# RWKV in units of 128 tokens on two lanes in place of 256 on one, in a two-layer hybrid decoder

## The chip, the cores and the metric

The kernel runs on one core of a Trainium2 chip. The metric is device time in microseconds of that core: the median of several executions of the whole program. A core has TensorE (PE in the profile: a row for matmuls and one, PEld, for the weight loads that overlap them), VectorE (DVE), ScalarE (ACT), GpSimd (POOL) and the queue SP that issues the DMAs. Each engine works off its own list of instructions in order; semaphores make it wait for the others. TensorE runs at one of two levels, 1.2 or 2.4 GHz; the profile's "granted clock" is the mean share of the higher one.

## The reference: what is computed

Two decoder layers run over a prompt of 2,048 tokens and over a sample group of 8 sequences of 8 tokens that shares the weights. A layer projects the normed input once and hands parts of it to four recurrent mixers (retention, HGRN, GLA, RWKV-7), each with four heads of 64. Their gated outputs are joined, go through `w_out`, and a cross attention to 256 memory tokens follows.

```python
def mixer(h, l, pos, st, v_first, P):
    proj = h @ P['w_in'][l]
    p_ret, p_hgrn, p_gla, p_rwkv = jnp.split(proj, ...)
    ...
    out = jnp.concatenate([o_ret, o_hgrn, o_gla, o_rwkv], axis=-1) @ P['w_out'][l]

def rwkv7_scan(r, w, k, v, kk, a, s0):     # S is (heads, 64 values, 64 keys)
    def step(S, inp):
        rt, wt, kt, vt, kkt, at = inp
        sa = jnp.einsum('bhvk,bhk->bhv', S, kkt)
        S = (S * wt[:, :, None, :] - sa[..., None] * (kkt * at)[:, :, None, :]
             + vt[..., None] * kt[:, :, None, :])
        return S, jnp.einsum('bhvk,bhk->bhv', S, rt)
```

The change cuts the prompt's RWKV recurrence into other pieces; the recurrence itself stays.

## The kernel before

The prompt is worked off in blocks of 512 tokens, four to a layer. In this text block 1.2 is layer 1, block 2; there are eight, from 0.0 to 1.3. In each layer the first block also carries projections of the sample, its RWKV and its GLA, the second block its HGRN, retention and gates (`TURN`).

**Stages of a block.** `block` projects the RWKV inputs, runs RWKV (`R_rwkv`), projects and runs GLA, HGRN and retention; `gates` projects the gates; `finish` multiplies by `w_out` and does the cross attention. The projections and `w_out` are the dense matmuls: 24 to a PSUM tile, 128 rows by 512 or 256 columns, in 32-bit words split into a high and a low part (the tiles `whl`, `act`, `oh`, `ol`). Weights come from DRAM for each block.

**RWKV.** `R_rwkv` takes a unit of 256 tokens, two units to a block, one after the other: they share the tiles of the pool `wk1`, which has one buffer for each name. Inside a unit the tokens lie in chunks of 64. A run of elementwise work on DVE and ACT makes the decays and keys; `invert` inverts the chunks' triangular matrices by doubling in four levels; then come the chunk products and a short serial chain over the chunks through the state `H`. One level of `invert` is: PE transposes `X`; ACT and DVE copy `X` into the block-diagonal tile `Xb` (L947, L949); PE multiplies (`Xb,XB`); ACT and DVE copy the product out of PSUM into `Wb`; PE multiplies (`Wb,XB`); DVE writes `X` under a mask (L968). A unit of 256 tokens has 8 such matrices side by side, so `X` is 128x256.

**PSUM.** Eight banks are four pools of two: `psd` for the dense matmuls, `psb` for GLA and HGRN, `psa` and `psc` for the rest. `PS` hands RWKV's tiles out by turns from `psa` and `psc` (lane `"ac"`).

**What sets the order.** A scheduler lists the instructions of each engine by priorities (`rank`, the table `PRI`) and readiness. `held` keeps a run of matmuls together: after each group's first it raises the priority of the next ones, up to 12 for the dense groups (`DENSE`) and 48 for all others (`SMALL`). So in the part of a block where RWKV runs, the engine lists interleave RWKV, GLA or HGRN on `psb`, and dense groups of the projections that come later in the block. A dense group that stands there is no longer there to be put beside later work.

Three lines carry the unit:

```python
        nu = 1 if smp else 2          # L996
            for u in range(NT // 2):  # L1372
                R_rwkv(l, pr, st["H"], rk, on["rwkv"], wk, u, vfb)
```

Of the kernel before, what the change touches and what calls it, by code (L numbers as in the profile page):

```python
# [12 lines left out]
I32 = mybir.dt.int32  # L13
# [31 lines left out]
SMALL = 48  # L45
# [12 lines left out]
def shape_constants(seq, past):  # L58
# [69 lines left out]
    c["reset"] = np.broadcast_to((np.arange(256) % 64 != 0).astype(f), (128, 256)).copy()  # L128
    c["resets"] = np.broadcast_to((np.arange(SN) % SL != 0).astype(f), (128, SN)).copy()
    return c  # L130


@with_exitstack
def decoder(ctx, tc, I, C, O):
# [74 lines left out]
    run = [SMALL, 0, None]  # L209
# [183 lines left out]
    def group(out, pairs):  # L393
        n = len(pairs)
        run[:] = DENSE, 0, None
        for i, (a, b) in enumerate(pairs):
            mm(out, a, b, i == 0, i == n - 1)
        run[:] = SMALL, 0, None

# [196 lines left out]
    def outputs(seg, score, v, qd, S, NG, NC, kT, tot, wp, eps, center, evac, state_out=None):  # L596
# [316 lines left out]
    def invert(NA, smp, wp):  # L913
# [10 lines left out]
        pair = wp.tile([128, ng * 256], F32, name="XB", tag="kk")  # L924
        ND = pair[:P, :m * 32].rearrange("p (q n) -> p q n", q=m)
        XB = pair[:, m * 32:m * 32 + ng * P].rearrange("p (g b n) -> p g b n", g=ng, b=nb)
        out = wp.tile([128, m, 64], F32, name="XT", tag="wt2")
        flat = lambda x: x.rearrange("p q n -> p (q n)")
        four = lambda x, g: x[:, 4 * g:4 * g + 4]
# [13 lines left out]
        def diagonal(dst, src, n):  # L943

            for b in range(n):
                if b % 2:
                    V.tensor_copy(dst(b), src(b))  # L947
                else:
                    A.activation(dst(b), src(b), AF.Copy)  # L949

        def turned():
            pt = PS("r")[:, :ng * P]
            for g in range(ng):
                tr(pt[:, g * P:(g + 1) * P], flat(four(X, g)), P)
            diagonal(lambda b: Xb[blk[b], :, b, :], lambda b: X[blk[b]], nb)
            A.activation(XB.rearrange("p g b n -> p (g b n)"), pt, AF.Copy)
        for li in range(1, 3 if smp else 5):
            turned()
            pw = PS("r")[:, :ng * P].rearrange("p (g b n) -> p g b n", g=ng, b=nb)
            for g in range(ng):  # L960
# [3 lines left out]
            pz = PS("r")[:P, :m * 32].rearrange("p (q n) -> p q n", q=m)  # L964
            for g in range(ng):
                for b in range(nb):
                    mm(flat(four(pz, g))[blk[b]], XB[:, g, b, :], flat(Wb[:, g, b]))
            V.copy_predicated(X, bc(lmask[:P, li].unsqueeze(1), [P, m, 32]), pz)  # L968
# [6 lines left out]
        low = wp.tile([128, ng * 2, 64], F32, name="XL", tag="rx")  # L975
        G.tensor_copy(low[:, :, 32:64], bc(K["I32"].unsqueeze(1), [128, ng * 2, 32]))
        pw = PS("r")[:, :ng * 64].rearrange("p (g e n) -> p g e n", g=ng, e=2)
        for g in range(ng):
            for q in range(4):
                mm(pw[blk[q], g], NA[:, 4 * g + q, 0, 32:64], Xb[:, 4 * g + q, 0:4:2, :])  # L980
        for q in range(4):
            V.tensor_copy(Wb[blk[q], :, 1:4:2, q, :], XB[blk[q], :, 1:4:2, :])
        A.activation(low[:, :, 0:32], pw.rearrange("p g e n -> p (g e) n"), AF.Copy)
        pz = PS("r")[:, :m * 32].rearrange("p (q n) -> p q n", q=m)
        for g in range(ng):
            for e in range(2):
                mm(flat(four(pz, g))[64 * e:64 * e + 64], low[:, 2 * g + e, :], flat(Wb[:, g, 2 * e + 1]))
# [3 lines left out]
    def R_rwkv(l, seg, Hst, d, on, wp, hb, vf):  # L991
# [4 lines left out]
        nu = 1 if smp else 2  # L996
        P = 64 * ne
        n = nu * P
# [151 lines left out]
        if not smp:  # L1150
            Z = wp.tile([128, m, 2, 64], F32, name="Z", tag="EA")
            A.activation(Z[:, :, 1, :], pk, AF.Copy)
            ps = PS("t").rearrange("p (u i g d) -> p u i g d", u=nu, i=2, g=2)
            for u in range(nu):
                for i in range(2):
                    tr(ps[:, u, i].rearrange("p g d -> p (g d)"), al[:, i, u * 128:(u + 1) * 128], 128)
            A.activation(Z[:, :, 0, :].rearrange("p (g q) d -> p g q d", g=2), ps.rearrange("p u i g d -> p g (u i) d"), AF.Copy)
# [4 lines left out]
            for p in range(2):  # L1162
                A.activation(U[:, p * nq:(p + 1) * nq].rearrange("p q a b -> p q (a b)"), ps[p], AF.Copy)
# [882 lines left out]
```

## Time and profile before

| | us |
|---|---|
| median of three executions (lowest, highest) | 3620.43 (3615.89, 3628.23) |
| the profiled execution, its own time | 3610.52 |
| its span, first to last instruction | 3608.7 |
| PE busy | 3342.4 (93%) |
| PEld busy | 2834.0 (79%) |
| DVE busy | 2069.8 (57%) |
| ACT busy | 1254.4 (35%) |
| POOL busy | 538.4 (15%) |

The mean granted clock over the span is 0.956. A block takes between 350 and 520 us. The text cuts each block in three: the **RWKV stretch** (on PE, from the first low-rank matmul of RWKV, `sm,w` or `dn_v,rwv`, to the transposes of RWKV's last output tile, `fpack,wosb`), the **middle** (from there to the first `w_out` matmul, `whl,oh`: what is left of GLA, HGRN, retention, the sample and the gates) and the rest. Busy times are unions of the instructions' spans, and the end of a matmul is modelled, so a busy PE need not be PE at its peak.

### The profile page before, as it was taken

To read this page: it belongs to the slowest core of one execution; us is meant where nothing else is said; L and a number is where in the kernel's file an instruction comes from. 1 tells how busy PE (TensorE), PEld (TensorE's weight loads), DVE (VectorE), ACT (ScalarE), POOL (GpSimd) and SP (SyncE) were. 2 spreads that over 40 slices of the span, in tenths; PEclk is the share of its full clock that TensorE was granted. 3 is DMA by queue.
4 is the path that set the end of the run, shared out by engine and by line. 5 is a ranking of instruction groups with operands and counts; after the bars stand their busy time and mean duration, and the time that the engine had idled before them with its cause. 6 is when DMAs were issued, how large, how long until landed. Compare 5 with 4: busy or idle time off the path is not lost.

```text
span 3608.7 us, 85093 instructions
## 1 busy us (share of the span) xinstructions
PE 3342.4 (93%) x36126; PEld 2834.0 (79%) x36126; DVE 2069.8 (57%) x5631; ACT 1254.4 (35%) x2655; POOL 538.4 (15%) x632
## 2 busy tenths in 40 slices
PE   7898899999999999999999987999979999999998
PEld 5777687777978888888877856878868788877887
DVE  5665654775436744575456456467653467446754
ACT  4442234322243324332344323443322433244323
POOL 3313230111000100011122232211100011000100
PEclk8999799999999999999999977999989999999999
DMA  6424464236552254325543352542545522543255
GB/s 191 169 88 143 119 228 173 86 90 216 194 196 98 82 193 152 124 73 198 173 172 110 119 156 99 207 145 97 146 150 205 170 98 99 192 148 115 81 201 188
DMA packets 241952, 530.74 MB, mean 147 GB/s; under 512 B 66854, under 2 KB 179750, under 8 KB 197542
## 3 DMA queue, kind: packets, MB, share of 16 engines
q1 hardware_dynamic: 241574, 525.31, 42.6%
q8 instruction: 285, 4.67, 0.5%
q14 instruction: 93, 0.76, 0.1%
HBM read 410.10 MB, written 115.16 MB: 146 GB/s over the span
## 4 chain that ended last, share of the span: by engine, by line
PE 71%; DVE 17%; ACT 5%; issue 4%; DMA 3%; POOL 2%; SPq 0%; ACTq 0%; POOLq 0%; DVEq 0%
PE psd L221 38%; PE psa L221 12%; PE psc L221 11%; PE psb L221 4%; PE psa L263 2%; PE psb L263 2%; PE psc L263 2%; DVE rsq L227 1%; DMA wraw<-in_w_in 1%; DVE Sx L622 1%; POOL whl L227 1%; DVE hss L552 1%; DVE sT L755 1%; DVE osb L227 1%; DVE wosb L227 1%
## 5 line engine op out<-in xcount | busy, mean ns | idle before, releaser
L221 PE MATMUL psd<-act,whl 128*128 128x512 f32 (+1 forms) x4032 | 1014.0, 405 | 29.1 <-DVE th L1283 11.9
L221 PEld LDWEIGHTS psd<-act,whl 128*128 128x128 f32 (+1 forms) x4032 | 751.6, 191 | 211.4 <-issue 22.2
L221 PE MATMUL psd<-whl,act 128*128 128x256 f32 x3840 | 537.7, 293 | 12.3 <-POOL whl L227 8.1
L221 PEld LDWEIGHTS psd<-whl,act 128*128 128x128 f32 x3840 | 487.3, 195 | 38.2 <-issue 16.4
L227 POOL TENSOR_TENSOR whl<-wraw,whl 128x1024 fp32r<-128x1024 f32 (+1 forms) x90 | 216.0, 2406 | 354.3 <-ACT whl L349 343.9
L271 POOL TENSOR_TENSOR ri<-ri,mhalf 128x1 f32<-128x1 f32 (+1 forms) x87 | 49.8, 573 | 1129.0 <-DVE ri L270 1116.1
L221 PE MATMUL psd<-whl,oh 128*128 128x256 f32 x1152 | 211.4, 284 | 0.0
L221 PEld LDWEIGHTS psd<-whl,oh 128*128 128x128 f32 x1152 | 177.7, 189 | 1.1 <-issue 0.3
L221 PE MATMUL psd<-whl,ol 128*128 128x256 f32 x576 | 162.7, 283 | 0.0
L349 ACT ACTIVATE whl<-wraw 128x1024 fp32r<-128x1024 f32 (+1 forms) x90 | 94.2, 1048 | 104.5 <-PE psc L221 35.5
L949 ACT ACTIVATE Xb<-X 32x256 f32<-32x256 f32 (+1 forms) x164 | 67.6, 412 | 143.1 <-DVE X L968 101.8
L221 PE MATMUL psb<-dn_hq,dn_hf 64*64 64x32 f32 (+1 forms) x3840 | 86.4, 234 | 30.9 <-DVE dn_hq L227 9.7
L221 PEld LDWEIGHTS psb<-dn_hq,dn_hf 64*64 64x64 f32 x3840 | 76.1, 149 | 46.8 <-issue 37.8
L221 PEld LDWEIGHTS psd<-whl,ol 128*128 128x128 f32 x576 | 108.6, 189 | 0.0
L227 DVE TENSOR_TENSOR x<-x,psd 128x256 f32<-128x256 f32 x72 | 30.3, 421 | 129.4 <-PE psd L221 129.4
L227 POOL TENSOR_TENSOR tot<-tot 128x8 f32<-128x8 f32 (+7 forms) x128 | 37.4, 293 | 409.1 <-DVE dn_gq L227 179.3
L426 ACT ACTIVATE xs<-xn 128x1024 f32<-128x1024 f32 (+1 forms) x34 | 35.9, 1055 | 173.4 <-PE psb L263 143.8
L755 DVE COPY_PREDICATED sT<-upack,psb 128x256 f32<-128x256 uint8 (+1 forms) x200 | 76.7, 428 | 30.6 <-PE psb L221 29.2
L1283 DVE SCALAR_TENSOR_TENSOR th<-th,psd 128x512 f32<-128x512 f32 x48 | 32.3, 686 | 95.1 <-ACT th L1282 95.0
L221 PEld LDWEIGHTS psd<-hts,wraw 128*64 128x64 f32 x1984 | 67.8, 141 | 20.3 <-issue 9.1
L221 PE MATMUL psa<-whl,oh 128*128 128x256 f32 x448 | 82.8, 283 | 0.0
L221 PE MATMUL psc<-whl,oh 128*128 128x256 f32 x448 | 82.7, 282 | 0.0
(776 smaller groups left out, 6844.7 us busy)
## 6 DMA issues: line engine op xcount, KB each, us to landing
whl<-w_w_out SPq DMA_DIRECT2D x56, 1024.0 KB
wraw<-in_w_in SPq DMA_DIRECT2D x76, 512.0 KB
wraw<-in_w_out SPq DMA_DIRECT2D x32, 512.0 KB
w_w_out<-whl SPq DMA_DIRECT2D x16, 1024.0 KB
x<-x SPq DMA_DIRECT2D x32, 512.0 KB
whl<-w_rw_r SPq DMA_DIRECT2D x12, 1024.0 KB
whl<-w_rw_k SPq DMA_DIRECT2D x12, 1024.0 KB
whl<-w_rw_v SPq DMA_DIRECT2D x12, 1024.0 KB
```

The source lines that it names most:

```text
L221: PE.matmul(out, lhsT=lhsT, rhs=rhs, start=start, stop=stop, skip_group_check=True)
L227: e.tensor_tensor(out, a, b, op)
L263: PE.transpose(out, in_, ident[:rows, :rows])
L271: G.tensor_tensor(y, y, mhalf[:P], ALU.pow)
L349: A.activation(hl[:, 0], raw, AF.Copy)
L426: A.activation(out, xt, AF.Square, accum_out=ss[:P])
L552: V.tensor_reduce(ss[:P, :n4], sq[:P, :n4], AX.X, ALU.add)
L622: V.scalar_tensor_tensor(b, a, tot(t, c)[gs], pu[gs, t, c, :], ALU.mult, ALU.add)
L755: V.copy_predicated(out, bc(mk, [P, w, 32 // s, s]), ps)
L949: A.activation(dst(b), src(b), AF.Copy)
L1283: V.scalar_tensor_tensor(th, th, 1.0, x, ALU.add, ALU.mult)
```

## The change

RWKV's unit becomes 128 tokens, four to a block. The units take turns on two lanes: `Turn` gives unit u the tiles and the PSUM pool of lane u % 2 (`psa` or `psc`), each tile half as large as before, so two units can be under way at a time. Their only dependence is the state `H`, which a unit reads near its end. `invert` has 4 matrices in place of 8. `SMALL` goes: all runs of matmuls are held by 12. In the blocks with the sample the state slot `Sx` of GLA and HGRN moves from the mixers' pools into the tile `th` of `dnp`. GLA, HGRN and retention keep their units of 512 (256 in the blocks with the sample).

```diff
-SMALL = 48
...
-    c["reset"] = np.broadcast_to((np.arange(256) % 64 != 0).astype(f), (128, 256)).copy()
+    c["reset"] = np.broadcast_to((np.arange(128) % 64 != 0).astype(f), (128, 128)).copy()
...
+class Turn:
+    def __init__(self, pool, i):
+        self.pool, self.i = pool, i
+
+    def tile(self, shape, dtype, name, tag, bufs=None):
+        return self.pool.tile(shape, dtype, name=name, tag=f"{tag}{self.i}", **({"bufs": bufs} if bufs else {}))
...
-    run = [SMALL, 0, None]
+    run = [DENSE, 0, None]
...
+            elif center:
+                x = wp.tile([128, nt - 1, NC, 128], F32, name="Sx", tag="Sx")
             else:
-                x = wp.tile([128, nt - 1, NC, 128], F32, name="Sx", tag="Sx")
+                x = dnp.tile([128, TB], F32, name="Sx", tag="th", bufs=2)[:, :NC * 128].rearrange("p (t c n) -> p t c n", t=1, c=NC)
...
-        m = NA.shape[1]
-        ng = m // 4
...
-        pair = wp.tile([128, 2, m, 32], F32, name="X", tag="wt1")[:P]
+        pair = wp.tile([128, 2, 4, 32], F32, name="X", tag="wt1")[:P]
...
-            pw = PS("r")[:, :ng * P].rearrange("p (g b n) -> p g b n", g=ng, b=nb)
-            for g in range(ng):
-                for q in range(4):
-                    mm(flat(pw[:, g])[blk[q]], ND[:, 4 * g + q, :], flat(Xb[:, 4 * g + q]))
-            diagonal(lambda q: Wb[blk[q], :, :, q, :], lambda q: pw[blk[q]], 4)
+            pw = PS("r")[:, :P].rearrange("p (b n) -> p b n", b=nb)
+            for q in range(4):
+                mm(flat(pw)[blk[q]], ND[:, q, :], flat(Xb[:, q]))
+            diagonal(Wb, pw, 4)
...
-        nu = 1 if smp else 2
-        P = 64 * ne
-        n = nu * P
+        nu = 1
+        P = n = 64 * ne
...
-            for j in range(ng):
+            for j in range(2):
                 ph = PS("r")[:, :128].rearrange("p (i n) -> p i n", i=2)
...
-            for u in range(NT // 2):
+            for u in range(NT):
+                wp = Turn(wk, u % 2)
                 vfb = None
                 if l > 0:
-                    vfb = wk.tile([128, 2, 256], F32, name="vfb", tag="vT")
-                    dma(vfb, vf[b][:, :, u * 256:(u + 1) * 256])
-                R_rwkv(l, pr, st["H"], rk, on["rwkv"], wk, u, vfb)
+                    vfb = wp.tile([128, 2, 128], F32, name="vfb", tag="vT")
+                    dma(vfb, vf[b][:, :, u * 128:(u + 1) * 128])
+                with on_lane("ac"[u % 2]):
+                    R_rwkv(l, pr, st["H"], rk, on["rwkv"], wp, u, vfb)
```

The engine lists move at three places that the prediction speaks of. In the rows, `fpack,X` is a transpose of `X`, `dn_gq` and `dn_gk` are GLA, `dn_hq`, `dn_hf`, `dn_hv` are HGRN, `Ss`, `sv`, `vx` and `ds_` tiles are the sample, `whl` with `act` is dense; the last number is how many stand in a row.

DVE, one level of `invert` in block 0.1, before:

```order
L947 COPY Wb<-psc 32x8x32 x2
L968 COPY_PREDICATED X<-upack,psa 128x256
L947 COPY Xb<-X 32x8x32 x2
L755 COPY_PREDICATED sT<-upack,psb 128x8x2x16 x2
L227 TENSOR_TENSOR dn_gk<-dn_gk,tot_13403 128x16x16
L227 TENSOR_TENSOR dn_gq<-dn_gq,tot_13403 128x32x16
L947 COPY Wb<-psa 32x8x32 x2
L968 COPY_PREDICATED X<-upack,psc 128x256
L947 COPY Xb<-X 32x8x32 x2
```

and after:

```order
L956 COPY Wb<-psa 32x4x32
L956 COPY Xb<-X 32x4x32 x2
L766 COPY_PREDICATED sT<-upack,psb 128x8x4x8
L956 COPY Wb<-psa 32x4x32
L766 COPY_PREDICATED sT<-upack,psb 128x8x4x8
L956 COPY Wb<-psc 32x4x32
L236 TENSOR_TENSOR dn_gk<-dn_gk,tot_14717 128x32x8
L236 TENSOR_TENSOR dn_gq<-dn_gq,tot_14717 128x64x8
L956 COPY Wb<-psc 32x4x32
L974 COPY_PREDICATED X<-upack,psa 128x128
L974 COPY_PREDICATED X<-upack,psc 128x128
L975 STREAM_TRANSPOSE X<-X 128x128
```

Where one matrix set of 128x256 went through, two of 128x128 go through, with twice the copies and the two lanes' steps mixed.

PE, two levels of the same `invert`, before:

```order
L221 MATMUL psc<-Wb,XB 32x128 x8
L221 MATMUL psb<-dn_gq,dn_gk 64x64 x16
L263 MATMUL psa<-fpack,X 128x128 x2
L221 MATMUL psc<-Xb,XB 32x128 x8
L221 MATMUL psd<-act,whl 128x512 x12
L221 MATMUL psa<-Wb,XB 32x128 x8
L221 MATMUL psb<-dn_gq,dn_gk 64x128 x8
L263 MATMUL psc<-fpack,X 128x128 x2
```

and after:

```order
L230 MATMUL psd<-act,whl 128x512 x12
L272 MATMUL psa<-fpack,X 128x128
L230 MATMUL psa<-Xb,XB 32x128 x4
L230 MATMUL psc<-Wb,XB 32x128 x4
L230 MATMUL psb<-dn_gq,dn_gk 64x64 x14
L272 MATMUL psc<-fpack,X 128x128
L230 MATMUL psc<-Xb,XB 32x128 x4
L230 MATMUL psb<-dn_gq,dn_gk 64x64 x2
L230 MATMUL psd<-act,whl 128x512 x12
L230 MATMUL psa<-Wb,XB 32x128 x4
L230 MATMUL psc<-Wb,XB 32x128 x4
L230 MATMUL psb<-dn_gq,dn_gk 64x64 x14
```

Before, the pools `psa` and `psc` alternate within one unit; now each is a unit of its own, the groups are half as long, and a transpose is followed at once by its own lane's product.

PE in the middle of block 1.0, the second half of HGRN, before:

```order
L221 MATMUL psb<-dn_hq,dn_hf 64x32 x64
L263 MATMUL psa<-fpack,osb 128x128 x4
L221 MATMUL psb<-dn_hq,dn_hf 64x32 x16
L221 MATMUL psb<-dn_hq,dn_hf 64x64 x8
L263 MATMUL psb<-fpack,dn_hf 128x128 x4
L221 MATMUL psb<-dn_hv,ha 64x64 x8
L221 MATMUL psb<-S_hgrn,dn_hq 64x128 x2
L221 MATMUL psb<-dn_hv,sT 64x64 x4
```

and after:

```order
L230 MATMUL psc<-Ss,qx 64x64 x10
L230 MATMUL psa<-vx,gmn 32x512 x2
L230 MATMUL psb<-dn_hq,dn_hf 64x64 x8
L272 MATMUL psa<-fpack,dn_rk 128x128 x4
L230 MATMUL psa<-vx,gmn 32x512 x2
L230 MATMUL psd<-whl,act 128x256 x12
L272 MATMUL psb<-fpack,dn_hf 128x128 x4
L230 MATMUL psd<-whl,act 128x256 x12
L272 MATMUL psc<-fpack,osb 128x64 x2
L230 MATMUL psb<-dn_hv,ha 64x64 x8
```

Before, this half stands behind the sample's mixers with retention alone beside it; now it ends beside the sample's GLA (`vx,gmn`), ahead of retention, with dense groups between.

## Rows read from the trace of the kernel before

**Rows 1.** The page's busy times: engine, us, share, instructions.

```profile
PE 3342.4 (93%) x36126; PEld 2834.0 (79%) x36126; DVE 2069.8 (57%) x5631; ACT 1254.4 (35%) x2655; POOL 538.4 (15%) x632
```

**Rows 2.** Windows: eight RWKV stretches; length, engines' busy us, clock, DMA share, GB/s.

```profile
123.00:299.00 176.00, 160.28 (x2329) 135.71 (x2328) 113.89 (x311) 71.32 (x151) 41.13 (x40) 0.96 0.31 113
620.00:778.00 158.00, 151.19 (x2525) 127.82 (x2524) 115.04 (x321) 63.73 (x135) 13.78 (x28) 1.00 0.23 81
1080.00:1247.00 167.00, 160.46 (x2620) 137.79 (x2617) 117.53 (x337) 58.47 (x128) 17.66 (x30) 1.00 0.23 80
1461.00:1618.00 157.00, 150.71 (x2518) 127.11 (x2517) 114.09 (x321) 63.59 (x135) 14.45 (x30) 1.00 0.23 81
1865.00:2061.00 196.00, 181.29 (x2534) 155.19 (x2534) 122.31 (x336) 77.86 (x163) 48.78 (x43) 0.97 0.34 121
2380.00:2572.00 192.00, 181.96 (x2752) 157.52 (x2750) 134.67 (x382) 72.21 (x150) 21.55 (x37) 0.99 0.32 111
2864.00:3051.00 187.00, 179.37 (x2752) 155.77 (x2751) 133.88 (x377) 67.63 (x144) 21.41 (x36) 1.00 0.29 100
3249.00:3438.00 189.00, 180.84 (x2744) 156.11 (x2742) 136.14 (x377) 70.16 (x146) 20.64 (x34) 0.99 0.28 94
```

**Rows 3.** Windows of the eight middles, in the order of the blocks.

```profile
299.00:489.00 190.00, 158.44 (x1681) 126.86 (x1680) 120.83 (x329) 55.16 (x112) 63.26 (x63) 0.83 0.45 140
778.00:905.00 127.00, 115.80 (x1039) 95.79 (x1039) 74.88 (x233) 27.09 (x56) 22.15 (x26) 0.92 0.65 197
1247.00:1328.00 81.00, 76.90 (x519) 65.67 (x518) 49.33 (x129) 23.46 (x41) 6.72 (x9) 0.98 0.57 198
1618.00:1717.00 99.00, 91.22 (x639) 78.93 (x639) 51.34 (x140) 20.71 (x35) 13.06 (x17) 0.98 0.59 195
2061.00:2248.00 187.00, 151.86 (x1500) 116.90 (x1501) 108.81 (x317) 53.89 (x112) 54.34 (x57) 0.72 0.39 123
2572.00:2691.00 119.00, 93.94 (x833) 73.11 (x834) 61.34 (x184) 23.03 (x50) 16.30 (x21) 0.83 0.51 153
3051.00:3117.00 66.00, 60.85 (x399) 50.37 (x400) 38.34 (x97) 19.46 (x35) 4.82 (x7) 0.95 0.51 184
3438.00:3502.00 64.00, 60.98 (x417) 51.21 (x417) 36.17 (x89) 16.85 (x28) 4.26 (x6) 1.00 0.53 191
```

**Rows 4.** Groups by form: DVE and ACT; count, busy us, mean ns, idle before.

```profile
L227 DVE TENSOR_TENSOR bn<-bn,EA 128x512 f32<-128x512 f32 x16 | 10.9, 682 | 0.0
...
L227 DVE TENSOR_TENSOR ar<-kk,eb 128x256 f32<-128x256 f32 x32 | 13.1, 416 | 0.0
...
L1116 ACT ACTIVATE kT<-psa 128x512 f32<-128x512 f32 x8 | 4.8, 596 | 18.9 <-PE psa L263 14.9 <-issue 4.1
L956 ACT ACTIVATE XB<-psa 128x256 f32<-128x256 f32 x40 | 15.3, 382 | 5.0 <-PE psa L263 4.2
```

**Rows 5.** Chain of waits in `w_out`: start, us, what.

```profile
1357.79 2.85 PE psd L221 x24
1360.64 1.43 PE psa L221 x12
```

**Rows 6.** The same chain inside an RWKV stretch, block 0.3.

```profile
1489.35 1.62 PE psd L221 x12
```

**Rows 7.** Window in block 1.3 with the densest DVE found over 60 us.

```profile
3355.00:3415.00 60.00, 55.72 (x1010) 49.97 (x1007) 53.09 (x149) 24.64 (x56) 7.66 (x12) 1.00 0.23 78
```

**Rows 8.** The chain in the middle of block 1.0, second half of HGRN.

```profile
2202.39 1.14 PE psb L221 x32
2203.52 0.47 DVE sT L755 x2
2203.99 0.33 DVE dn_hf L227
2204.33 0.34 DVE dn_hq L227
```

**Rows 9.** Waits of PE over the whole run: us in total, times, longest.

```profile
PE psc L263 <- DVE osb L227: 13.6, 5, 7.7
```

More of the change, by code (lines that the diff above doesn't have):

```diff
@@ L394, in group @@
         n = len(pairs)
-        run[:] = DENSE, 0, None
+        run[2] = None
         for i, (a, b) in enumerate(pairs):
             mm(out, a, b, i == 0, i == n - 1)
-        run[:] = SMALL, 0, None
+        run[2] = None
     def dense_c(w, act, ps):
@@ L974, in invert @@
         turned()
[L975 to L980, printed above, removed]
-        for q in range(4):
[L982 to L987, printed above, removed]
+        low = wp.tile([128, 2, 64], F32, name="XL", tag="rx")
+        G.tensor_copy(low[:, :, 32:64], bc(K["I32"].unsqueeze(1), [128, 2, 32]))
+        pw = PS("r")[:, :64].rearrange("p (e n) -> p e n", e=2)
+        for q in range(4):
+            mm(pw[blk[q]], NA[:, q, 0, 32:64], Xb[:, q, 0:4:2, :])
+        for q in range(4):
+            V.tensor_copy(Wb[blk[q], 1:4:2, q, :], XB[blk[q], 1:4:2, :])
+        A.activation(low[:, :, 0:32], pw, AF.Copy)
+        pz = PS("r")[:, :128].rearrange("p (q n) -> p q n", q=4)
+        for e in range(2):
+            mm(flat(pz)[64 * e:64 * e + 64], low[:, e, :], flat(Wb[:, 2 * e + 1]))
         A.activation(out[:, :, 32:64], pz, AF.Copy)
@@ L1150, in R_rwkv @@
         if not smp:
-            Z = wp.tile([128, m, 2, 64], F32, name="Z", tag="EA")
+            Z = wp.tile([128, 4, 2, 64], F32, name="Z", tag="EA")
             A.activation(Z[:, :, 1, :], pk, AF.Copy)
[L1153 to L1157, printed above, removed]
@@ L1162, in R_rwkv @@
-            for p in range(2):
-                A.activation(U[:, p * nq:(p + 1) * nq].rearrange("p q a b -> p q (a b)"), ps[p], AF.Copy)
+                    mm(ps[ep, 2 * p + q, :], XT[ep, 2 * p + i, :], Z[ep, 2 * p + q].rearrange("p a b -> p (a b)"))
+            A.activation(U.rearrange("p q a b -> p q (a b)"), ps, AF.Copy)
             R1 = wp.tile([128, 2, n], F32, name="R1", tag="kp")
-            GT = wp.tile([128, 2, ng, 64], F32, name="GT", tag="kk")
-            DB = wp.tile([128, 2, ng, 64], F32, name="DB", tag="rx")
@@ new lines, in R_rwkv @@
+            ipe = [(i, p, e, slice(64 * p, 64 * p + 64), slice(64 * e, 64 * e + 64)) for i in range(2) for e in range(2) for p in range(2)]
+            for i, p, e, hp, ep in ipe:
+                mm(pr[e][hp, i], U[ep, 2 * p + i, 0, :], NA[ep, 2 * p + i, 1:3, :])
+            r4 = lambda x: x.rearrange("p i (e n) -> p i e n", e=2)
+            for e in range(2):
+                tt(V, GT[:, :, e], pr[e][:, :, 1, :], bc(K["I64"].unsqueeze(1), [128, 2, 64]), ALU.add)
+                tt(V, r4(R1)[:, :, e], pr[e][:, :, 0, :], r4(rt)[:, :, e], ALU.add)
@@ new lines, in R_rwkv @@
+            for e in range(2):
+                pg.append(PS("r")[:, :128].rearrange("p (i n) -> p i n", i=2))
+            for i, p, e, hp, ep in ipe:
+                mm(pg[e][hp, i, :], kT[ep, 0, hs(i, p)], vT[ep, 0, hs(i, p)], True, False)
+                mm(pg[e][hp, i, :], bT[ep, 2 * p + i, :], U[ep, 2 * p + i, 1, :], False, True)
+            for e in range(2):
+                tt(V, DB[:, :, e], pg[e], bc(eb[:, :, e, 64:65], [128, 2, 64]), ALU.mult)
+            Hn = wp.tile([128, 2, 2, 64], F32, name="Hn", tag="wt2")
@@ L1184, in R_rwkv @@
             V.tensor_copy(Hn[:, 0], Hst)
-            H = [Hn[:, j] for j in range(ng)] + [Hst]
-            for j in range(ng):
+            H = [Hn[:, 0], Hn[:, 1], Hst]
+            for j in range(2):
                 ph = PS("r")[:, :128].rearrange("p (i n) -> p i n", i=2)
@@ L1234, in R_rwkv @@
         if not smp:
-            o4 = lambda x: x.rearrange("p u (i g n) -> p u i g n", i=2, g=2)
-            pq = [PS("r")[:, :nu * 128].rearrange("p (u i n) -> p u i n", u=nu, i=2) for _ in range(2)]
+            o4 = lambda x: x[:, 0].rearrange("p (i g n) -> p i g n", i=2, g=2)
+            pq = [PS("r")[:, :128].rearrange("p (i n) -> p i n", i=2) for _ in range(2)]
             for q, i, u, e, tk, hp, ep in each(0):
@@ L1637, in w_out @@
                     for t in ts:
-                        run[:] = DENSE, 0, None
                         for n, k in enumerate(ks):
```

73 lines of the change are left out of this document (31 added, 42 removed).

## The prediction, as it was put on record

> **What bounds the kernel now.** I read the page's busy times first [rows 1]: PE is busy 93% of the span and no other engine over 60%, so a change pays if it takes work or waiting off PE. Then I cut every block in three and read windows. In the RWKV stretches [rows 2] the reader is to see that PE is already full: in block 0.2 it is busy 160.5 of 167 us at a granted clock of 1.00, while DVE is busy 117.5. The eight stretches sum to 1422 us (176, 158, 167, 157, 196, 192, 187, 189). The time that PE loses lies elsewhere, in the middles of three blocks that carry the sample [rows 3]. In 1.0 PE is idle for 35 of 187 us and its granted clock is 0.72, so that it ran there partly at 1.2 in place of 2.4 GHz, worth another 52 us (187 x 0.28); in 0.0 the same reading gives 32 and 32 of 190, in 1.1 it gives 25 and 20 of 119. The chain of waits names one cause: the second half of HGRN runs behind the sample, and one of its levels is 1.1 us of small matmuls and then 1.2 us of DVE in which PE has nothing [rows 8]; the 1.1 middle has two long waits for a retention output on DVE, up to 7.7 us [rows 9]. So two halves of a unit that overlap can give little inside the RWKV stretch, where dense groups hide its chain already; what they can give is that the stretch needs fewer dense groups to hide it and leaves them to the middles.
>
> **DVE and ACT: more instructions, the same elements.** By the instruction lists DVE gets 1,496 more, all of RWKV, 187 to a block; ACT gets 760, or 95 to a block. A DVE instruction of 512 elements takes 682 ns and one of 256 takes 416 [rows 4], so one cut in two costs 2 x 416 - 682 = 150 ns more. That is 28 us of DVE in each RWKV stretch, 224 in all. On ACT it is 2 x 382 - 596 = 168 ns, 16 us to a stretch; ACT is busy at most 78 of some 190 us there [rows 2], so I cost that at nothing, and without that cover it would be 16 us to a block. DVE's busy time in the stretches goes from 114, 115, 118, 114, 122, 135, 134, 136 to 142, 143, 146, 142, 150, 163, 162, 164, in sum 1212. How full can DVE be when its list is in order and it waits for PE and ACT? Over a whole stretch it is 0.70 to 0.72 in blocks like 1.2 and 1.3; over the densest 60 us that I found it is 53.1, or 0.885 [rows 7]. With two units and GLA or HGRN to choose from I take the upper end, which gives 160, 162, 165, 160, 169, 184, 183, 185 us as DVE's floors.
>
> The Trainium skill bears on this in its page "Perfetto Trace Analysis", section "Optimizing Scalar/DVE Operations", which argues both ways: larger grouped operations help where the engine is saturated, while breaking instructions up may help where it is not but makes others wait. It puts the fixed cost on SBUF at about 60 ns of engine time and says that the profiled latency is about twice that. The rows' 150 ns is near the double; with 60 ns the stretches would get 11 us of DVE each, DVE would be no floor anywhere, and RWKV would end some 20 us lower in sum. The row decides here.
>
> **PE: the same columns, more switches, other neighbours.** Matmul counts hardly move (112 more, each of them half of one that is gone), so the work is the same. Three things move. First, the dense groups that stand in the RWKV stretches. A dense matmul of 256 columns takes 0.119 us (12 in 1.43) [rows 5], one of 512 is counted double. Counted so, the stretches lose 120, 24, 24, -36, 228, 156, 144, 132 of them, or 14, 3, 3, -4, 27, 19, 17, 16 us, 94 in sum, to the middles. Second, the lists have 409 more rows in the stretches and 161 more in the middles, which is 409 and 161 more changes from one group to another. A change costs nothing in `w_out`, where 12 take 1.43 whatever came before [rows 5], and up to 0.19 in an RWKV stretch, where 12 dense matmuls take 1.62 [rows 6]. I take 0.10, about the middle, since only part of the new changes are beside dense groups: 41 us and 16 us. Third, the half-size groups wait on half-size copies, and `X` is followed at once by its own product; that wait is already in the stretches of before, so I give it no term. PE's floors are then length less what leaves plus the changes: 168, 160, 168, 166, 174, 179, 176, 178.
>
> **The RWKV stretches in sum.** The larger floor of each is 168, 162, 168, 166, 174, 184, 183, 185, in sum 1390. Both engines are now near full and each waits for the other in a fixed order, so I add 4 us to each stretch, somewhat over half of the 6.5 that PE is idle in 0.2 now [rows 2]: 1422. Against 1422 before, that is no change: what leaves, 94 us, is paid back by DVE's floor, the changes and the waiting. The bounds are 1372, if changes and waiting cost nothing, and 1683, if DVE stays at 0.72.
>
> **The middles.** In 1.0 the second half of HGRN ends ahead of retention and beside dense groups, so its own 35 us or so of half-idle time go, and 27 us of dense work come in, into a middle that loses 87 us (35 idle and 52 of clock). Between nothing and the 60 us that are left after that work is placed, I take half, -30; by the same rule 0.0 (64 lost, 14 come in, 50 left) gets -25. In 1.1 the 19 that come in fit into the 45 lost, and dense groups now stand by retention, so I take -8, about half of the two long waits. In 0.1 (10 of clock, 11 idle) and 0.2 (6 in all) the 3 that come in are hidden. 0.3 gives 4 away. In 1.2 and 1.3 the middles are full, losing 8 and 3 us [rows 3], so of 17 and 16 some 9 and 13 us are left over on the path. The changes add 11 outside the terms of 0.0 and 1.0. Sum: -30 - 25 - 8 - 4 + 9 + 13 + 11 = -34. The rest of each block, `w_out` and the cross attention, keeps its order. What `SMALL` did is in the row counts; the moved `Sx` slot takes a tile of the gates and has free time around it, which I cost at nothing; if it made the second HGRN half wait, that is the second rival. The weights that the moved dense groups need are 1 MB for 24 groups and move with them, in middles where the DMA engines are busy 0.39 and 0.45 in 1.0 and 0.0 [rows 3].
>
> **The time.** The profiled execution took 3610.5 us, 10 us under the median of 3620.4. 3610.5 + 0 - 34 = 3576, and beside the median 3586: I say 3585.
>
> **Rivals.** (1) *DVE takes PE's place, slower.* If DVE reaches not 0.85 of the stretches, which the forecast needs (1212 of 1422), but 0.80, halfway between 0.72 and 0.885 [rows 2, 7], the stretches take 1515, 93 more, and the total is +59: 3670 in the profile, 3680 as a median. It decides from a DVE share under 0.83 (1212 / 1456). For it: every unit now runs all its DVE steps in order with the other lane's, and PE's list cannot fill what it did not foresee. Against it: three chains feed DVE where there were two. The page "Perfetto Trace Analysis" of the Trainium skill, in the section named above, warns of this case. Chance 0.32. (2) *The middles hold.* The sample's RWKV, GLA and retention follow each other as before; if they, and not HGRN, set the end in 0.0 and 1.0, only 20 of the 55 us come, and the total is +1: 3611, median 3620. Against it stands the half-idle stretch [rows 8], for it that the sample's chain has no less work. Chance 0.13. (3) *More than forecast.* Changes cost nothing and the two engines never wait for each other: stretches 1372, middles -45, in all -95: 3515, median 3525. For it, `w_out` pays nothing [rows 5]; against it, 1.62 in place of 1.43 [rows 6]. Chance 0.12. The forecast keeps 0.43.
>
> **How the numbers follow.** A measurement of this kernel can tell about 0.3%, 11 us, from no change. The forecast is faster but for 0.03, so faster is 0.40 + 0.12 = 0.52; same is 0.13 and 0.01 of the forecast, 0.14; slower is 0.32 and 0.02, 0.34. The range reaches from 3505, under the third rival's median, to 3695, over the first rival's; beyond it lie DVE shares under 0.79 and a fuller recovery of the middles.
>
> **What would show it.** In the changed profile: DVE busy some 2290 us in all, ACT some 1380; the eight RWKV stretches together near 1422 us with DVE at 0.85 in them; the middles of 1.0 and 0.0 near 157 and 165 us with the clock there over 0.9; the middles of 1.2 and 1.3 some 10 us longer. The forecast is wrong if the stretches sum to over 1456, with PE idle waiting for `X`, `Xb` or `Wb`, or if the middle of 1.0 keeps its low clock.

## The result: slower by half a per cent, and the profile after

The changed kernel takes 3635.4 us, the median of eleven executions; the kernel before takes 3615.9 over eleven that stand beside them. The ratio is 1.0053, with a 95% interval of 1.0039 to 1.0067. The forecast was 3585 and faster.

The page of the changed kernel, busy times (engine, us, share, instructions), against [rows 1]:

```profile
PE 3415.0 (94%) x36350; PEld 2846.7 (78%) x36350; DVE 2267.3 (62%) x7127; ACT 1371.9 (38%) x3415; POOL 554.6 (15%) x712
```

DVE gained 197 us and ACT 118, close to the forecast (2267 where 2290 was said, 1372 for 1380). The next two fences are windows of the changed kernel, in the columns of [rows 2, 3]. First the RWKV stretches of 1.0 and 1.3, and the sum over all eight:

```profile
1878.00:2069.80 191.80, 172.72 (x2303) 135.69 (x2300) 145.60 (x520) 87.06 (x252) 39.75 (x54) 0.87 0.27 91
...
3267.70:3446.60 178.90, 169.07 (x2515) 137.08 (x2514) 143.66 (x514) 80.68 (x237) 19.91 (x42) 1.00 0.25 88
sum 1408.70, PE 1329.15 PEld 1068.84 DVE 1114.34 ACT 634.35 POOL 190.61; mean PE 166.14 PEld 133.60 DVE 139.29 ACT 79.29 POOL 23.83
```

Then the middles of 0.0, 1.0, 1.2 and 1.3, and the sum over all eight:

```profile
300.40:484.70 184.30, 164.08 (x1804) 136.40 (x1803) 123.95 (x322) 58.73 (x117) 65.44 (x60) 0.91 0.47 153
...
2069.80:2256.00 186.20, 166.42 (x1776) 137.51 (x1774) 124.21 (x326) 59.45 (x120) 64.38 (x59) 0.88 0.46 148
...
3052.30:3137.10 84.80, 79.44 (x542) 67.46 (x541) 47.02 (x125) 22.65 (x40) 7.54 (x10) 0.98 0.53 189
3446.60:3536.80 90.20, 85.27 (x686) 72.84 (x685) 50.35 (x144) 20.77 (x35) 6.45 (x8) 1.00 0.45 161
sum 989.90, PE 905.58 PEld 760.31 DVE 613.98 ACT 269.20 POOL 207.45; mean PE 113.20 PEld 95.04 DVE 76.75 ACT 33.65 POOL 25.93
```

The stretches went from 1422 to 1409, the middles from 933 to 990. In 1.0 the clock of the middle rose from 0.72 to 0.88, and the middle is still as long as it was (187 to 186); the stretch ahead of it, at 0.97 before, is now at 0.87.

The experiments are easiest to read by two groups of blocks. The table gives stretch and middle together, from each run's own profile: the two blocks with the sample's RWKV (0.0, 1.0), and the six plain ones. "Room" is explained with e18. A profile is one execution, up to 12 us from its kernel's median, and the kernel before itself has medians from 3611.6 to 3618.3 in the rounds of measurement, so a few us between two rows decide nothing.

| kernel | lanes | hold | room for HGRN | median us | two sample blocks | six plain blocks |
|---|---|---|---|---|---|---|
| before | 1 | 48 | no | 3616 | 749 | 1607 |
| e2 | 1 | 12 | no | 3614 | 734 | 1629 |
| e18 | 1 | 48 | mask | 3580 | 716 | 1602 |
| e3 | 1 | 48 | slot | 3570 | 700 | 1617 |
| e5 | 1 | 12 | slot | 3562 | 690 | 1628 |
| e12 | 1 | 12, HGRN 48 | slot | 3554 | 689 | 1615 |
| e20 | 1 | 12, HGRN 48 | mask | 3549 | 691 | 1610 |
| e15 | 1 | 12, HGRN 48 | no (own tile) | 3597 | 724 | 1616 |
| e19 | 2 | 12 | no | 3644 | 746 | 1649 |
| e6 | 2 | 48 | mask | 3595 | 724 | 1625 |
| e13 | 2 | 12 | mask | 3594 | 696 | 1649 |
| e1 | 2 | 48 | mask, slot | 3595 | 720 | 1626 |
| **changed kernel** | 2 | 12 | mask, slot | 3635 | 742 | 1656 |
| e11 | 2 | 12, HGRN 48 | mask, slot | 3586 | 708 | 1628 |
| e14 | 2 | 12 | mask, own tile | 3595 | 698 | 1650 |
| e16 | 2 | 12, HGRN 48 | mask, own tile | 3592 | 716 | 1624 |

### The profile page after: what moved, and what is told of

Same layout as the page of the kernel before. It is cut to its first block, busy times and chain, and to the rows that moved or that the text cites. A ratio compares the mean times of both kernels' runs of the same rounds, so it can differ in the third digit from the quotient of the medians.

```text
span 3644.3 us, 88156 instructions
## 1 busy us (share of the span) xinstructions
PE 3415.0 (94%) x36350; PEld 2846.7 (78%) x36350; DVE 2267.3 (62%) x7127; ACT 1371.9 (38%) x3415; POOL 554.6 (15%) x712
## 4 chain that ended last, share of the span: by engine, by line
PE 67%; DVE 20%; ACT 4%; issue 3%; DMA 3%; POOL 2%; SPq 0%; ACTq 0%; POOLq 0%; DVEq 0%
PE psd L230 34%; PE psa L230 12%; PE psc L230 11%; PE psb L230 5%; PE psc L272 2%; PE psa L272 2%; DVE rsq L236 2%; PE psb L272 2%; DVE Sx L633 1%; DVE osb L236 1%; DVE hri L292 1%; DVE Wb L956 1%; DVE hss L561 1%; DVE Xb L956 1%; POOL whl L236 1%
## 5 line engine op out<-in xcount | busy, mean ns | idle before, releaser
L230 PE MATMUL psd<-act,whl 128*128 128x512 f32 (+1 forms) x4032 | 998.6, 401 | 19.3 <-DVE carry L539 7.8
L230 PE MATMUL psd<-whl,act 128*128 128x256 f32 x3840 | 551.0, 296 | 3.8 <-ACT whl L358 1.6
L958 ACT ACTIVATE Xb<-X 32x128 f32<-32x128 f32 x324 | 99.3, 307 | 125.3 <-DVE X L974 75.7
L230 PE MATMUL psb<-dn_hq,dn_hf 64*64 64x32 f32 (+1 forms) x3840 | 119.8, 225 | 9.1 <-DVE dn_hq L236 4.1
L230 PEld LDWEIGHTS psb<-dn_hq,dn_hf 64*64 64x64 f32 x3840 | 104.0, 138 | 28.8 <-issue 18.2
L230 PE MATMUL psd<-hts,wraw 128*64 128x64 f32 x1984 | 84.4, 232 | 1.9 <-DVE th L1285 1.9
L956 DVE COPY Xb<-X 32x128 f32<-32x128 f32 x324 | 79.3, 246 | 7.6
```

The costliest lines, as they stand in the source:

```text
L230: PE.matmul(out, lhsT=lhsT, rhs=rhs, start=start, stop=stop, skip_group_check=True)
L956: V.tensor_copy(o, i)
L958: A.activation(o, i, AF.Copy)
```

## The experiments

**One part at a time (e1 to e4).** First the theories were that short holds cut GLA's and HGRN's runs (S), or that the lanes cost the time (L).

e1 puts the long holds back:

```diff
-    run = [DENSE, 0, None]
+    run = [SMALL, 0, None]      # SMALL = 48; group() sets DENSE and back, as before
```

> The changed kernel with one part undone: runs of small matmuls are held by 48 again, as before the change (PE's list has 6,357 rows; 6,553 in the changed kernel, 5,985 before). Theory S (the splitting of GLA's and HGRN's runs costs the time): in the changed kernel the matmuls of dn_gq,dn_gk and dn_hq,dn_hf take 23.4 us more of PE than before (179.8 against 156.3, from start to start); held by 48 they go back to some 157, and the median falls from 3635 to 3605-3618. Theory L (the lanes cost it, by halved groups that end more often: X, Xb and Wb take 35 us more of PE): the median stays within 8 us of 3635, since PE fills what it gains with waiting for DVE.

Measured: 3594.7, ratio to the kernel before 0.9946 (0.9924 to 0.9968). That is 41 us under the changed kernel, below the range of S and far from that of L.

e2 is the kernel before with the short holds alone, the reverse of that edit.

> The kernel before with that one part alone: all runs of matmuls held by 12, units of 256 on one lane. Theory S: dn_gq,dn_gk and dn_hq,dn_hf take some 20 us more of PE, and the median goes from 3616 to 3630-3640, which is all of the change's loss. Theory L: within 8 us of 3616, because shorter holds also let RWKV's small groups in sooner.

Measured: 3614.4, ratio 0.9994 (0.9976 to 1.0013): nothing, in the range of L. So the holds cost 41 us beside the other parts (e1) and nothing by themselves (e2); neither S nor L says both.

e3 is the kernel before with `Sx` in the `th` tile, as in the diff of the change.

> The kernel before with only the slot Sx of the blocks with the sample moved into a tile of the gates. If the slot is what lets the second half of HGRN stand earlier, the middles of 0.0 and 1.0 (190 and 187 us) get shorter by 5 to 25 us each and the median falls to 3580-3608. If the lanes are what moves it, nothing changes: 3616, within 8 us.

Measured: 3569.9, ratio 0.9885 (0.9849 to 0.992). The part that I had costed at nothing is worth 1.2% alone.

e4 takes the overlap away and keeps the halves:

```diff
-                wp = Turn(wk, u % 2)
+                wp = Turn(wk, 0)
-                with on_lane("ac"[u % 2]):
+                with on_lane("ac"):
```

> The changed kernel with its units of 128 on one lane (the tiles of lane 0 for every unit, PSUM from the two pools by turns as before): halved instructions without overlap. If the overlap is what the halves buy, four serial chains stand in each RWKV stretch where two stood, the stretches (1409 us in sum in the changed kernel) grow by 60 us or more, and the median is 3690 or above. If DVE's count of instructions or PE's changes set the time and not the chains, it stays within 20 us of 3635.

Measured: 4005.3, ratio 1.1075. The eight stretches take 2015 us in sum. In e5 below, which has the same holds and slot and units of 256 on one lane, they take 1377: 86 us to a unit of 256, and here 63 to a unit of 128 (at a mean granted clock of 0.906 over the span, against 0.972). So half the tokens are far from half the time on one lane, and the second lane buys back what the halves lose. Busy times of e4:

```profile
PE 3513.4 (88%) x36350; PEld 2911.7 (73%) x36350; DVE 2270.7 (57%) x7127; ACT 1384.3 (35%) x3415; POOL 549.9 (14%) x712
```

DVE does the same work in e4 as in the changed kernel (2267) and is busy for a smaller share of the span: it waits, it is not full.

**Parts in pairs, and DVE's instructions (e5, e6, e7, e10).** e5 is e3 with the short holds.

> Units of 256 on one lane, with the slot Sx moved and all runs held by 12: the changed kernel without its lanes. Measured so far: the slot alone 3570, holds of 12 alone 3614 against 3612, and with lanes and slot the holds cost 41 us (3595 to 3635). If it is the lanes that make the short holds dear (more groups to change to), this takes 3562-3582. If it is the slot (HGRN then stands beside RWKV, and it is HGRN's long runs that are cut), it takes 3598-3618.

Measured: 3562.4, ratio 0.9854 (0.9827 to 0.9881). That is the range of the lanes: one lane bears short holds with the slot moved, too.

e6 is the changed kernel with long holds and `Sx` back in the mixers' pools.

> The lanes alone: units of 128 on two lanes, runs held by 48, Sx in the mixers' pools as before. If the parts add up, the lanes cost the 25 us here that they cost with the slot moved (3570 to 3595), and this takes 3627-3647. If what I forecast for the lanes holds (they let the second half of HGRN stand earlier and fill the middles of 0.0 and 1.0), it takes 3575-3595.

Measured: 3594.5, ratio 0.9943 (0.9922 to 0.9964). This looked like my forecast for the lanes come true; e19 speaks against it.

e7 is e3 with a wrapper around VectorE in the prompt's RWKV that writes each elementwise operation, copy and transpose of 64 elements or more as two:

```diff
+            for h in range(2):
+                f(out[..., half h], *[the same half of each operand], **k)
```

> The kernel before with Sx moved (3570), and each DVE operation of the prompt's RWKV written as two of half the size: 1,144 more DVE instructions, about 172 us more of DVE's busy time at 0.15 each, PE's matmuls and their groups unchanged. If DVE's added instructions are what the lanes cost, this loses most of the lanes' 25 us: 3585-3600. If the cost is on PE (groups cut in half, X, Xb and Wb ending 133 times where they ended 68), DVE's time is hidden: 3562-3578.

Measured: 3602.0, ratio 0.9956 (0.994 to 0.9971), 32 us over e3 and just above the range of DVE's instructions. Busy times of e3 and then of e7:

```profile
PE 3322.0 (93%) x36126; PEld 2820.1 (79%) x36126; DVE 2080.6 (58%) x5631; ACT 1253.4 (35%) x2655; POOL 536.1 (15%) x632
```

```profile
PE 3339.4 (93%) x36126; PEld 2827.8 (79%) x36126; DVE 2164.1 (60%) x6775; ACT 1255.9 (35%) x2655; POOL 538.9 (15%) x632
```

1,144 more instructions made DVE busy for 84 us more, 73 ns each. By the blocks, the loss is in the two with the sample (700 to 728) and in what follows the middles (1127 to 1136); the six plain ones take 1614 against 1617. So more DVE instructions cost nothing in the plain blocks, where dense groups cover the chain, and they are hardly what the lanes cost there. That they delay a chain with little beside it in the sample blocks is my reading of these times; no run shows it.

e10 has the lanes in blocks 0.1 and 1.1 alone:

```diff
+            two = b == 1
+            nu = 1 if two else 2
-            for u in range(NT // 2):
+            for u in range(NT // nu):
+                wp = Turn(wk, u % 2) if two else wk
```

> The kernel before with Sx moved, and the lanes of 128 in blocks 0.1 and 1.1 alone (units of 256 on one lane in the other six, runs held by 48). Lanes with the slot made 0.1 and 1.1 shorter by 5.5 and 5.3 us and 1.0 and 1.3 longer by 18 and 11 (3595 in all against 3570). If the lanes' worth hangs on the block, this takes 3552-3566, under both kernels and under the slot alone; if those block differences are only work handed on to the next block, it takes 3566-3580.

Measured: 3564.0, ratio 0.9854 (0.9833 to 0.9876), in the range of "the block matters". The interval overlaps that of e3, so the 6 us stay inconclusive.

**The slot beside the lanes (e11 to e16).** e11 holds the prompt's HGRN by 48 in the changed kernel; e12 does the same in e5.

```diff
+                run[0] = 48
                 R_hgrn(l, gr, st["hgrn"], ...)
+                run[0] = DENSE
```

> The changed kernel with the prompt's HGRN alone held by 48 again, all else by 12 (PE's list has 86 rows of dn_hq,dn_hf; 153 in the changed kernel, 93 with every run held by 48). Between these two the matmuls of dn_hq,dn_hf took 75.7 us of PE with long holds and 117.5 with short ones, 42 us, which is all of the 41 us between 3595 and 3635. If HGRN's cut runs are the loss, this takes 3585-3605. If the loss is that short holds no longer let RWKV end sooner once it has two lanes, and HGRN only shows it, this stays at 3620-3640.

> Units of 256 on one lane, Sx moved, holds of 12 for all but HGRN's 48. There short holds made the RWKV stretches 38 us shorter (1416 to 1378) and the middles 40 us longer, with 31 us more for dn_hq,dn_hf. If HGRN's cut runs are what the middles pay, the two can be parted and this takes 3525-3550, the best of all. If the middles grow because what leaves the stretches has to stand somewhere, it stays at 3555-3575.

Measured: e11 3586.3, ratio 0.9937 (0.9913 to 0.9961); e12 3553.8, ratio 0.9841 (0.9822 to 0.9859). Both moved the way of the cut runs, e11 into that range, e12 to a place between its two ranges. The matmuls of HGRN in the page's groups (count, busy us, mean ns, idle before), of e11 and of the changed kernel:

```profile
L230 PE MATMUL psb<-dn_hq,dn_hf 64*64 64x32 f32 (+1 forms) x3840 | 77.4, 222 | 8.2 <-DVE dn_hq L236 4.6 <-DVE dn_hf L851 2.1 <-issue 1.0
```

```profile
L230 PE MATMUL psb<-dn_hq,dn_hf 64*64 64x32 f32 (+1 forms) x3840 | 119.8, 225 | 9.1 <-DVE dn_hq L236 4.1 <-DVE ds_qk L236 2.7 <-DVE dn_hf L851 1.7
```

e13 is the changed kernel with `Sx` back in the mixers' pools.

> The changed kernel with Sx back in the mixers' pools: lanes and short holds without the slot. With long holds the slot was worth nothing beside the lanes (3594.5 without, 3594.7 with it). If that holds with short ones, this takes 3627-3643, like the changed kernel; if the slot's 46 us are still in it, 3660 or more.

Measured: 3594.2, ratio 0.9959 (0.9941 to 0.9976). Its HGRN matmuls take 118.4 us, as cut up as in the changed kernel, and it is 41 us faster, outside both ranges. So the cut runs are not the whole loss, and the slot costs 41 us where one lane gained 42 from it (e3, against the kernel before in its own round). The two profiled executions are 53 us apart, 46 of them in the two sample blocks (742 against 696). With the old slot the short holds cost nothing beside the lanes either (e6 3594.5, e13 3594.2): 24 us more in the plain blocks, 28 less in the sample's.

What the slot does is in the trace of 1.0. ACT's first writes of `th` by HGRN's query projection (L532), and the last writes of GLA's state (the fields after the durations are first and last start); first the changed kernel, then e13:

```profile
L532 ACT ACTIVATE th<-psd x4: 224/408/597, 2029.0 to 2046.2; 128x512 f32<-128x512 f32 x2, 128x64 f32<-128x64 f32 x2
L633 DVE SCALAR_TENSOR_TENSOR S_gla<-Sx,tot,psb x4: 272/280/288, 1950.1 to 2031.5; 64x64 f32<-64x64 f32 x4
```

```profile
L532 ACT ACTIVATE th<-psd x4: 224/411/599, 1975.0 to 1996.4; 128x512 f32<-128x512 f32 x2, 128x64 f32<-128x64 f32 x2
L631 DVE SCALAR_TENSOR_TENSOR S_gla<-Sx,tot,psb x2: 273/280/286, 2004.9 to 2005.2; 64x64 f32<-64x64 f32 x2
```

There are two `th` tiles. GLA's keys `dn_gk` hold one, its `Sx` now holds the other, and the projection, whose PSUM tile is read through `th`, has to wait for GLA: it writes 2 us ahead of GLA's end in the changed kernel and 30 us ahead of it otherwise. The dense groups behind it wait with it: from 100 to 150 us into the stretch of 1.0 PE runs 44 of the prompt's dense matmuls in the changed kernel and 88 in e13. Windows of the changed kernel there, 10 us each, and of e13 at the same distance from the start of the stretch (columns as in [rows 2]):

```profile
1998.00:2008.00 10.00, 8.85 (x98) 6.03 (x96) 7.37 (x20) 3.08 (x11) 3.32 (x4) 0.83 0.25 105
2008.00:2018.00 10.00, 8.84 (x113) 4.40 (x109) 8.30 (x29) 6.26 (x19) 1.35 (x2) 0.50 0.20 54
2018.00:2028.00 10.00, 7.62 (x95) 5.29 (x95) 6.90 (x23) 5.92 (x20) 2.21 (x5) 0.50 0.26 107
```

```profile
1976.00:1986.00 10.00, 8.29 (x136) 6.05 (x136) 8.48 (x31) 4.05 (x16) 0.85 (x4) 1.00 0.37 133
1986.00:1996.00 10.00, 9.62 (x153) 6.75 (x152) 7.44 (x29) 7.89 (x26) 3.67 (x6) 1.00 0.36 129
1996.00:2006.00 10.00, 9.90 (x186) 7.99 (x186) 7.95 (x26) 4.89 (x15) 2.39 (x1) 1.00 0.38 149
```

A granted clock of 0.50 is the lower level, 1.2 GHz. The chain of waits in that stretch of the changed kernel shows both lanes' `invert` with nothing beside it (start, us, what):

```profile
2013.18 0.47 PE psa L272
2013.65 0.59 PE psc L230 x8
2014.24 0.48 PE psa L230 x8
...
2014.80 0.28 ACT Wb L958
...
2015.10 0.28 DVE Wb L956
...
2015.42 0.31 DVE Wb L956
...
2015.77 0.65 PE psc L230 x8
2016.43 0.70 PE psa L230 x8
```

e14 tests this: the slot stays out of the mixers' pools but shares nothing.

```diff
-                x = dnp.tile([128, TB], F32, name="Sx", tag="th", bufs=2)[:, :NC * 128]...
+                x = dnp.tile([128, 256], F32, name="Sx", tag="Sx")[:, :NC * 128]...
```

> The changed kernel with Sx still out of the mixers' pools, but in a tile of its own (one buffer of 128x256) in place of one of the two th tiles. In the trace of the changed kernel, block 1.0, HGRN's query projection first writes th at 2029, two us before GLA's second half lets go of its state (2031), and 37 us after the projection ahead of it; with Sx in the mixers' pools (3594) it does so at 1975, 30 us ahead of GLA's end. Theory T: GLA's Sx and dn_gk hold both th tiles until GLA ends, the dense groups behind that projection stand still, and RWKV's chain lies bare at half clock. Then a tile of its own gives back the 41 us: 3580-3602. If it is only the earlier start of HGRN beside two lanes that costs the time, it stays at 3620-3640.

Measured: 3594.8, ratio 0.9944 (0.9925 to 0.9963). The 41 us are back, so without the shared `th` there is no such loss. But sharing alone is not enough. e11 shares it too, and there the projection comes as late, 2.5 us ahead of GLA's end:

```profile
L532 ACT ACTIVATE th<-psd x4: 223/408/597, 2010.6 to 2027.9; 128x512 f32<-128x512 f32 x2, 128x64 f32<-128x64 f32 x2
L633 DVE SCALAR_TENSOR_TENSOR S_gla<-Sx,tot,psb x4: 271/280/289, 1934.2 to 2013.1; 64x64 f32<-64x64 f32 x4
```

The dense groups stand still there as well (42 of the prompt's dense matmuls in the same 50 us), yet its sample blocks take 708 us, between the 698 and 716 of the two kernels with a tile of its own (e14, e16 below). In the changed kernel 16 of the 46 us are in the stretches (371 against 355 in e13) and 30 in the middles (371 against 341). e11's middles take 344, so what is lost there goes with HGRN's cut runs: HGRN's second half leaves its state 292 us into block 1.0 (counted from the stretch's start), 276 in e13, 269 in e11, and retention and the gates follow it. How the late dense groups and the cut runs work on each other there is left open.

e15 and e16 put the same tile into e12 and e11.

> The fastest kernel so far (units of 256 on one lane, Sx moved, HGRN's runs held by 48 and all else by 12; 3554), with Sx in a tile of its own. Theory T: there too th is first written as late as GLA's end (in the run with the slot moved alone at 1961, GLA's end at 1966), so it gains a little, 3535-3550. If with one lane GLA ends early enough for dense groups not to run out, nothing changes: 3550-3560.

> The changed kernel with Sx in a tile of its own and HGRN's runs held by 48 (all else by 12): the two lanes with both troubles taken away. With the shared tile and long HGRN runs it took 3586, with the old slot and short runs 3594. If the two are separate losses (dense groups standing still in blocks 0.0 and 1.0; cut runs in all blocks), this takes 3545-3570. If they are the same one, it takes 3580-3595.

Measured: e15 3596.6, ratio 0.9955 (0.9938 to 0.9972), 43 us slower than e12, which no theory had; e16 3592.3, ratio 0.9953 (0.9935 to 0.9972), in the range of "the same one". In e16 the long runs save 26 us in the plain blocks (1650 to 1624) and lose 18 in the sample's; why 1.0 is longer there (370 against 349 us) is left open.

**Room (e18, e19, e20).** In e15 HGRN in 1.0 ran about as late as in the kernel before (its first operation `ha` 259 us after the stretch's start, 270 before, 127 in e12). A pool opens when its place in SBUF is free. By the kernel's own tile sizes 54.28 KB per partition are left beside the fixed tiles; the sample's RWKV takes 41.31 from one side, HGRN's pool in a sample block 13.00 from the other. That is 0.03 KB too much, so HGRN waits for the sample's RWKV. The slot out of the pool makes room (1 KB); in e15 the fixed tiles grow by that 1 KB, and it is gone again. The other source is one line of the change: `reset`, 128 columns wide in place of 256, frees 0.5 KB.

e18 is the kernel before with that line:

```diff
-    c["reset"] = np.broadcast_to((np.arange(256) % 64 != 0).astype(f), (128, 256)).copy()
+    c["reset"] = np.broadcast_to((np.arange(128) % 64 != 0).astype(f), (128, 128)).copy()
...
-            V.tensor_tensor_scan(cs[:, i, :], reset[:, :n], lw[:, i, :], 0.0, ALU.mult, ALU.add)
+            for q in range(0, n, P):
+                V.tensor_tensor_scan(cs[:, i, q:q + P], reset[:, :P], lw[:, i, q:q + P], 0.0, ALU.mult, ALU.add)
```

> The kernel before with one line of the change: the mask reset is 128 columns wide in place of 256 (the scan that reads it runs in two halves, 32 more DVE instructions in all). That frees 0.5 KB of SBUF per partition. Worked out from the pools' sizes: 54.28 KB are left beside the fixed tiles, the sample's RWKV takes 41.31, HGRN's pool in the blocks with the sample 13.00, together 0.03 KB too much, so HGRN there waits for the sample's RWKV to be done. Theory R (room): half a KB lets HGRN stand beside RWKV, as the slot's 1 KB did (3570), and this takes 3560-3580. If it is the slot's place that matters and not the room, it takes 3606-3620.

e19 is the changed kernel with the wide mask and the old slot.

> The changed kernel without any room gained: Sx in the mixers' pools and the mask 256 wide again, so that lanes and short holds are all that is left of the change. Theory R: HGRN stands behind the sample in 0.0 and 1.0 once more, and the 45 us or so that the lanes seemed to give (3594 with the narrow mask) are gone: 3625-3650. If the lanes themselves moved HGRN, it stays at 3590-3600.

Measured: e18 3580.4, ratio 0.9913 (0.989 to 0.9936); e19 3643.9, ratio 1.0091 (1.0076 to 1.0106). e18 is at the upper edge of theory R's range, e19 inside it. Room decides, on one lane and on two. In the trace of 1.0, HGRN's first operation (`ha`) and the sample's last one in RWKV (`ons_rwkv` on POOL), before and in e18:

```profile
L838 DVE TENSOR_SCALAR ha<-dn_hf,c,c x4: 398/404/413, 2134.7 to 2190.4; 128x256 f32<-128x256 f32 x4
L227 POOL TENSOR_TENSOR ons_rwkv<-ons_rwkv,og x1: 456/456/456, 2136.0 to 2136.0; 128x128 f32<-128x128 f32 x1
```

```profile
L838 DVE TENSOR_SCALAR ha<-dn_hf,c,c x4: 402/406/1884, 1966.4 to 2026.3; 128x256 f32<-128x256 f32 x4
L227 POOL TENSOR_TENSOR ons_rwkv<-ons_rwkv,og x1: 462/462/462, 2107.1 to 2107.1; 128x128 f32<-128x128 f32 x1
```

Before, HGRN starts just as the sample's RWKV ends; with half a KB more it starts 141 us ahead of that, beside the prompt's RWKV. With two lanes it is the same: in e19 HGRN starts 5 us before the sample's RWKV ends, in e13, which has half a KB more, 81 us before. Lanes with long holds and no room were not run.

e20 takes the room from the mask and adds e12's holds.

> Units of 256 on one lane with the narrow mask, Sx in the mixers' pools, HGRN's runs held by 48 and all else by 12. It differs from the fastest so far (3554) in where the room comes from: there Sx shared a th tile with HGRN's query projection, here nothing is shared. If the shared tile cost something on one lane too, 3535-3550; if GLA ends early enough there, 3550-3562. Above 3590 theory R falls.

Measured: 3548.9, ratio 0.9823 (0.9807 to 0.984). It beats both kernels, by 1.8% the one before, with units of 256 on one lane. Its interval overlaps that of e12, so whether the shared tile costs anything on one lane stays open.

## Why the prediction was wrong, point by point

**What bounds the kernel.** Right: PE is the bound, and what is to be had lies in the middles of the sample blocks. The cause that the rows named (HGRN behind the sample, [rows 8]) was right too; why it stood there I did not ask. It was room, and the changed kernel has it from the mask and the slot, not from the lanes.

**DVE.** The sum was right (2267 busy, 2290 forecast). The use of it was not: I left all of it in the stretches (1212), and 1114 stand there, a share of 0.79. DVE got 127 us more in the stretches and 73 more in the middles (541 to 614), where a part of HGRN went: the plain blocks' stretches have 2,956 of its matmuls in place of 3,696, and GLA's 2,232 as before. The floor of 0.85 was never met. The price of 150 ns was too high where it could be measured alone: 73 in e7. The Trainium skill's "Perfetto Trace Analysis", section "Optimizing Scalar/DVE Operations", puts it at about 60 ns of engine time; e7's 73 is near it, and in the changed kernel it is 132 (197.5 us by 1,496), with the other operands and waits that came along. By the page's figure the forecast would have been faster still, so this price is not the step that failed.

**The plain blocks.** By its own terms the forecast had 22 us more in their stretches and 21 more in their middles, 43 in all. Measured were 1607 to 1656, 49. Sum right, split wrong: the stretches became 14 us shorter and the middles 64 longer, since more work left the stretches than the dense groups that I counted (HGRN's 740 matmuls above); so the right sum is luck. The runs part these 49: about 18 from the lanes with long holds (e6 and e1 against the kernel before; against e18 and e3, with the same room, 23 and 9), some 24 to 30 from the short holds, of which HGRN's cut runs are 26 to 28 (e11, e16). I had put the cut runs into a count of rows at 0.10 us each. The count of matmuls was wrong too: PE has 224 more, not 112 (36,350 against 36,126), each half of one that is gone, so the columns are the same.

**The sample blocks, the step that failed.** The forecast was 22 us less in their stretches (168 and 174, and 4 of waiting in each, against 176 and 196) and 55 less in their middles, 77 in all. Measured were 749 to 742, 7 less. With the same lists but for the slot, e13, it is 53 less. The step was this: "the moved `Sx` slot takes a tile of the gates and has free time around it, which I cost at nothing; if it made the second HGRN half wait, that is the second rival". The tile isn't the gates' alone. HGRN's query projection goes through `th` some 120 us into the same stretch, and GLA's keys hold the other tile. The cost is 46 us in these two blocks, most of it in clock: they stand at the lower level for 157 us, against 75 in e13, and at half the rate up to 41 us of those 82 are lost (an estimate). I had also priced the slot by itself. It costs this only beside the short holds: with long ones it costs nothing (e6 3594.5, e1 3594.7), and the holds went into my sum as a count of rows alone. So either of them, taken back, gives back 41 us (e1, e13). The gain that e13 keeps is not the lanes' either: without the room of the mask it is gone (e19: 746).

**The rivals.** The second (the middles of 0.0 and 1.0 hold) named the place, and its 3620 is the nearest, but not the reason: HGRN's second half no longer waits for the sample (it starts 230 us after the stretch of 1.0 begins, 325 before), and the stretches there don't get shorter either. The first (DVE takes PE's place) did not happen: DVE's share, 0.79, is under the 0.83 from which it was to decide, yet the stretches are shorter than before, since less of DVE's work is in them; and in e7 the added instructions cost nothing in the plain blocks. The third had the direction of e13 and e14, and none of its terms.

**The signs to watch.** Neither sign came. The stretches sum to 1409, not over 1456. "The middle of 1.0 keeps its low clock" was named as what would make the forecast wrong. It rose to 0.88, and the low clock moved into the stretch ahead of it; I should have named the stretch as well.

## What to carry to other kernels

Ask of a moved buffer who else uses its ring between the first and the last use of the new tenant, above all whether a projection is read out through it: a dense group that can't be read out stops those behind it, and the chain that they covered lies bare. What that costs hangs on the rest of the order (742 us in the changed kernel, 708 in e11). Where the order of the work is set by pools, add up their sizes before and after: 0.03 KB too much kept a mixer behind another here, and freeing half a KB was worth 0.9% (e18), while the lanes and the short holds together cost 0.9% (e19). Parts of a change that do the same thing don't add up: the slot was worth 42 us alone, nothing beside lanes and mask with long holds, and minus 41 beside them with short ones.

## What the runs showed that I had not expected

Four serial chains of 128 tokens to a block take 2015 us in the eight stretches where two of 256 take 1422, or 1377 with the same holds and slot, with the same columns on PE (e4, e5). And holding matmuls in shorter runs makes PE busy for longer in the runs that are cut (HGRN from 77.4 to 119.8 us, though one matmul takes 222 and 225 ns: they stand back to back less often) without making the kernel slower by itself (e2, e5): in e2 the stretches get 50 us shorter and the middles 57 longer.
